# Three more weight slots from smaller rings, a gather moved behind the up product, and one branch for last passes and eviction, in a two-layer decoder trunk with a mixture of experts

## The chip, the cores and the metric

The kernel runs on one core of a Trainium2 chip. The metric is device time in microseconds: the median of the runs shown.

## The reference

Two layers; the second ends in a mixture of eight experts, of which each of 256 tokens takes two. The change touches how the expert part is run.

```python
D_MODEL, SEQ, DEPTH = 1024, 256, 2
N_EXPERTS, TOP_K, D_FF_EXPERT = 8, 2, 3584
...
def moe_swiglu(x, w_router, e_gate, e_up, e_down):
    ...
    logits = (t @ w_router).astype(jnp.float32)
    top_val, top_idx = lax.top_k(logits, TOP_K)
    top_w = jax.nn.softmax(top_val, axis=-1)
    gates = jnp.sum(jax.nn.one_hot(top_idx, N_EXPERTS, dtype=jnp.float32) * top_w[..., None], axis=1)
    out = jnp.zeros_like(t)
    for e in range(N_EXPERTS):
        out = out + gates[:, e:e + 1] * swiglu(t, e_gate[e], e_up[e], e_down[e])
    return out.reshape(B, S, D)

def reference(...):
    for layer in range(DEPTH):
        h = hybrid_mixer(x, ...)
        x = layer_norm(DEEPNORM_ALPHA * x + h, ...)
        f = swiglu(x, ...) if layer % 2 == 0 else moe_swiglu(x, ...)
        x = layer_norm(DEEPNORM_ALPHA * x + f, ...)
    return x
```

## The kernel before

All weights are float32 and come from HBM in **units** of 1 MB (128 partitions x 2048). `Stream` (name `W`) holds a plan of units in the order of use, and `NS` = 16 SBUF slots of one unit each, 18 in the expert part (`NX` = 2 more from a pool opened once the mixers' own tiles are gone). A unit is loaded into a slot (`load`, L169, on SP's queue, in order), and then `split` (L271, L272) writes it into two other slots: a rounded high part `h` by ScalarE (ACT) and the rest `l` = unit - h by VectorE (DVE). Products on TensorE (PE) use h and l in turn. `pump` decides after every step of the product loops (a `tick`; four to a unit) what is loaded and split: it splits a unit 12 ticks ahead of its use (`lead`), and it loads whenever more than 1 + max(0, freed + reserve - split) slots are idle, with reserve 5 in the expert part. So a spare slot goes to a load, not to a deeper lead of the splits. Slots come from a first-in first-out list.

An expert runs in four groups of hidden columns, 512, 1024, 1024, 1024 (the last expert the other way round). A group of 1024 has four units of gate, four of up, four of down. The first unit of each gate product is used unsplit (`whole`, L1050, against `xw`, the first half of the expert's tokens in plain float32). The order in the code is: gate product of group g, its eviction by ACT (`gated`, L1075), up product, its eviction (`finish`, L1085), and then the down product of the group *before* (`down`, L1137, L1144), so a group's hidden values have 13 ticks to be folded (L1108), activated (L1110), split (L1111 to L1113) and stored as `ch`, `cl`.

The routing is only known at run time. An expert with up to 64 tokens is narrow: its x holds high and low halves side by side in 128 columns, so that two matmuls per block do; one with more is wide and takes a third matmul (`rest`). Which one it is decides a branch (`cases`, L969) that PE, ACT and DVE all take. `last_passes` (L1032) is such a branch at the end of each pair of units; `gated` and `finish` are each another one right behind it.

Before expert e+1 starts, its tokens are picked from the residual `xf` by matmuls with a one-hot matrix: `one_hot` (L979 to L986, DVE), then `gather`: two transposes (L1012) and a copy to `pt` (L1014), then for each half of the model width a `pick` (L1000, PE), its split `exh`/`exl` (L991, L992), and the copy to `xw` (L1025). The whole is a task started after the down product inside group 2; it steps along with the ticks of the gate product of group 3. After an expert's last down product, `scatter` adds its result to `acc` (L1166 and L1167 on PE, L1169 on DVE); this falls into the first ticks of the next expert's group 1.

The numbers of tokens are such that experts 0 and 2 are wide and the other six narrow. PE starts expert 0's group 1 at 432.35 us, and the experts that follow at 536.8, 648.5, 774.5, 885.9, 995.0, 1104.5 and 1213.6 us.

Of the kernel before, what the change touches and what calls it, by code (L numbers as in the profile page):

```python
# [16 lines left out]
P = 128  # L17
# [12 lines left out]
NS = 16  # L30
NX = 2
NR = 6
# [7 lines left out]
def trunk(ctx: ExitStack, tc: tile.TileContext, x, w_in, gm_ws, gm_bs, gm_ln_g, gm_ln_b, gla_wa2, gla_ba,  # L40
# [26 lines left out]
    def tiny(name, n, dt=F32):  # L67
        return act.tile([P, n], dt, tag="tiny", name=name, bufs=10, padded_shape=[P, 32])

# [222 lines left out]
    def norm(y, st, gt, bt, nm):  # L292
# [85 lines left out]
    def transposed_parts(sg, nm, kt):  # L378

        tp = psw(f"th{nm}", (P, 4, P))  # L380
        for j in range(kt):
            nc.tensor.transpose(tp[:, j, :], sg[:, j * P:(j + 1) * P], ident)
        ch = act.tile([P, 4, P], F32R, tag="ch", name=f"ch{nm}", bufs=4)
        cl = act.tile([P, 4, P], F32R, tag="cl", name=f"cl{nm}", bufs=4)
        split(ch[:, 0:kt, :], cl[:, 0:kt, :], tp[:, 0:kt, :])
        return ch, cl
# [85 lines left out]
    def mixer(l, xT, small, ready, nxT):  # L472
# [354 lines left out]
    def moe(xT, ready, consts):  # L827
        iota, pri, ones, ecst, pair, fold, powers = consts
        lg = const.tile([P, 2, NE], F32, name="lg")
        plt = psy("plt", (P, 2, NE))  # L830
# [32 lines left out]
        small = const.tile([P, NE], F32, name="small")  # L863
        acc = [room[-1].tile([P, D], F32, name=f"acc{tb}") for tb in range(2)]

# [85 lines left out]
        class Expert:  # L951
# [22 lines left out]
            def one_hot(self):  # L974
                nm = self.nm
                self.oh = act.tile([P, 2, P], F32, tag="oh", name=f"oh{nm}", bufs=1)
                self.twice = self.oh
                for tb in range(2):
                    nc.vector.tensor_scalar(self.oh[:, tb, :], iota, self.rank(tb), None, op0=ALU.is_equal)  # L979
                if self.fewer is not None:  # L980
                    self.twice = s2(f"oh2{nm}", F32, (P, 2, P))
                    slot = s2(f"slot{nm}")[:, 0:P]
# [25 lines left out]
            def gather(self):  # L1008
# [5 lines left out]
                nc.scalar.activation(self.pt, tp, AF.Copy)  # L1014
                xh = act.tile([P, KT, P], F32R, tag="xh", name=f"exh{nm}")
                xl = act.tile([P, KT, P], F32R, tag="xl", name=f"exl{nm}")
                self.x = xh, xl
                for hf in range(2):
                    p = pst(f"gx{nm}{hf}", (P, 4, P))
                    self.pick(p, [xf[tb][:, hf * 512:hf * 512 + 512] for tb in range(2)])  # L1020
                    self.parts(xh[:, hf * 4:hf * 4 + 4, :], xl[:, hf * 4:hf * 4 + 4, :], p)
                    if hf == 0:
                        if self.wide is not None:
                            self.xw = room[-1].tile([P, 4, P], F32, tag="xw", name=f"xw{nm}", bufs=2)
                            nc.scalar.activation(self.xw, p, AF.Copy)  # L1025
                        yield 2

            def last_passes(self, rest, last):

                def run(ms):  # L1030
                    for ps, x, w, stop in ms:
                        nc.tensor.matmul(ps, x, w, start=False, stop=stop, skip_group_check=True)  # L1032
                self.cases(lambda: run(last), lambda: run([*rest, *last]))

            def product(self, units, n, nm):

# [4 lines left out]
                held, rest, last = [], [], []  # L1041
                for u, ((wh, wl), free, drop) in enumerate(units):
                    held.append(free)
                    for j in range(kk):
                        k = kk * u + j
                        for b in range(nb):
# [23 lines left out]
            def gated(self, pg, nm):  # L1070
# [8 lines left out]
            def finish(self, g, sg, pu, lag=13):  # L1079
                nm = f"e{self.nm}{g}"  # L1080
# [16 lines left out]
            def transposed(self, nm, sg, up):  # L1097

                tp = pst(f"th{nm}", (P, 4, P))
                ch = act.tile([P, 4, P], F32R, tag="ch", name=f"ch{nm}", bufs=4)  # L1100
                cl = act.tile([P, 4, P], F32R, tag="cl", name=f"cl{nm}", bufs=4)
                hid = room[-1].tile([P, 4, HALF], F32, tag="hid", name=f"hid{nm}", bufs=2)

# [91 lines left out]
        while W.hold:  # L1195
            tasks["route"].step()
        W.lead, W.reserve = LEAD_E, NC
        for i, t in enumerate((ybanks, ybanks, tbanks, tbanks)):
            t.append(psy(f"bank{i}"))

        def first_hidden():
            yield 4
            p = pst("gh", (P, 4, P))
            experts[0].pick(p, first, hidden_columns)
            ch = act.tile([P, 4, P], F32R, tag="ch", name="che0f", bufs=4)
            cl = act.tile([P, 4, P], F32R, tag="cl", name="cle0f", bufs=4)
            experts[0].parts(ch, cl, p)
# [7 lines left out]
        for e, ex in enumerate(experts):  # L1215
            for g, (c0, n) in enumerate(groups(e)):
# [4 lines left out]
                if (e, g) == (NE // 2, 1):  # L1221
                    most = nc.values_load(cnt_i[0:1, 0:1], min_val=0, max_val=2 * P)
                sg = ex.gated(ex.product(stream(gate_units(e, g)), n, f"eg{e}{g}"), f"e{e}{g}")
# [5 lines left out]
                pu = ex.product(stream(up_units(e, g)), n, f"eu{e}{g}")  # L1229
                task = Task(ex.finish(g, sg, pu, 3 if last else 13))  # L1230
                W.cap = len(W.plan) - 2 if last else len(W.plan)
# [17 lines left out]
        with tc.If(most > P):  # L1249
# [4 lines left out]
            with tc.For_i(0, NE) as ei:  # L1254
# [29 lines left out]
                for g in range(FE // 512):  # L1284
                    sg = ex.gated(ex.product(cols_of(exp_g, g), 512, f"egz{g}"), f"ez{g}")
                    pu = ex.product(cols_of(exp_u, g), 512, f"euz{g}")
                    Task(ex.finish(g, sg, pu)).finish()
                    ex.down(g, rows_of(g), g == 0, g == FE // 512 - 1)
# [112 lines left out]
```

## Time and profile before

| what | us |
|---|---|
| median of 3 runs | 1343.92 (1342.61 to 1344.07) |
| profiled execution, its own time | 1342.48 |
| its span, first to last instruction | 1340.8 |
| PE busy | 1296.5 (97%) |
| DVE busy | 1068.5 (80%) |
| ACT busy | 839.0 (63%) |
| mean HBM rate over the span | 318 GB/s |

A "PE busy" includes matmuls whose modelled ends overlap the next one's start, so PE's waits are read from the starts of its matmuls and from what the weight loads (PEld) and matmuls waited for. The mean granted TensorE clock is 0.996 of full speed. The expert part takes some 930 us of the span.

### The profile page before, as it was taken

The numbers are of one execution on the slowest core, as the hardware profiler recorded it, in microseconds if no ns is written. First come the engines' busy times: TensorE is split into PE (matmuls) and PEld (weight loads), VectorE is DVE, ScalarE is ACT, GpSimd is POOL, SyncE is SP. The second block draws the span as 40 slices with busy tenths as digits, with TensorE's granted clock in tenths as the row PEclk, the third lists the DMA queues.
The fourth block names the chain that finished last, engine by engine and source line by source line (L and its number), as shares of the span: only waits on it lengthen the run. The fifth ranks groups of instructions, "written<-read, shape, count | busy, mean of one in ns | idle before, by whom it ended". The sixth has DMA issues, their size and how long they took to land. (4 is left out here: it accounts for less than half of the span.)

```text
span 1340.8 us, 16964 instructions
## 1 busy us (share of the span) xinstructions
PE 1296.5 (97%) x6113; PEld 1024.0 (76%) x6113; DVE 1068.5 (80%) x965; ACT 839.0 (63%) x702; POOL 37.7 (3%) x79
## 2 busy tenths in 40 slices
PE   8999999999998999999999999999999999999996
PEld 7878888888887788777778877776776776777774
DVE  6687544476684887898888789899899989989997
ACT  5653444346342666687756667776777777877783
POOL 1012000000110000000000000000000000000000
PEclk9999999999999999999999999999999999999998
DMA  9636656543484598999999899999999999999993
GB/s 343 256 126 205 240 188 204 203 157 132 159 301 162 222 365 321 392 370 380 408 368 369 320 384 370 389 408 412 408 389 408 409 393 410 407 400 403 412 407 118
DMA packets 118766, 426.35 MB, mean 318 GB/s; under 512 B 8089, under 2 KB 10722, under 8 KB 104578
## 3 DMA queue, kind: packets, MB, share of 16 engines
q1 hardware_dynamic: 117218, 420.61, 81.0%
q0 software_dynamic: 1440, 4.33, 1.1%
q8 instruction: 64, 1.05, 0.3%
q14 instruction: 44, 0.36, 0.1%
HBM read 423.86 MB, written 1.05 MB: 317 GB/s over the span
## 5 line engine op out<-in xcount | busy, mean ns | idle before, releaser
L272 DVE TENSOR_TENSOR l<-r,h 128x2048 fp32r<-128x2048 f32 (+2 forms) x373 | 833.3, 2249 | 134.0 <-ACT h L271 117.6
L271 ACT ACTIVATE h<-r 128x2048 fp32r<-128x2048 f32 (+2 forms) x373 | 685.0, 1881 | 124.1 <-PE bank L1032 39.1
L1137 PE MATMUL bank<-h,che 128*128 128x512 f32 x440 | 174.4, 396 | 0.0
L1053 PE MATMUL eu<-h,exh 128*128 128x512 f32 x440 | 167.5, 389 | 0.0
L1144 PE MATMUL bank<-l,che 128*128 128x512 f32 x377 | 153.3, 407 | 7.0 <-DVEq L969 3.5
L1060 PE MATMUL eu<-l,exh 128*128 128x512 f32 x361 | 141.0, 391 | 0.3 <-DVE l L272 0.3
L1053 PE MATMUL eg<-h,exh 128*128 128x512 f32 x316 | 128.2, 418 | 0.0
L1050 PE MATMUL eg<-r,xw 128*128 128x512 f32 x248 | 114.5, 595 | 0.0
L1144 PEld LDWEIGHTS bank<-l,che 128*128 128x128 f32 x377 | 70.8, 188 | 41.9 <-DVE l L272 17.1
L1053 PEld LDWEIGHTS eu<-h,exh 128*128 128x128 f32 x440 | 82.6, 188 | 16.9
L1137 PEld LDWEIGHTS bank<-h,che 128*128 128x128 f32 x440 | 82.8, 188 | 15.2
L1060 PE MATMUL eg<-l,exh 128*128 128x512 f32 x237 | 92.7, 391 | 0.1
L1060 PEld LDWEIGHTS eu<-l,exh 128*128 128x128 f32 x361 | 67.8, 188 | 15.9 <-DVE l L272 2.1
L1050 PEld LDWEIGHTS eg<-r,xw 128*128 128x128 f32 x248 | 45.2, 190 | 39.6 <-issue 37.8
L266 PE MATMUL f<-h,xhm 128*128 128x512 f32 (+1 forms) x192 | 72.2, 376 | 0.0
L267 PE MATMUL f<-l,xhm 128*128 128x512 f32 (+1 forms) x192 | 71.4, 372 | 0.0
L268 PE MATMUL f<-h,xlm 128*128 128x512 f32 (+1 forms) x192 | 71.4, 372 | 0.0
L1053 PEld LDWEIGHTS eg<-h,exh 128*128 128x128 f32 x316 | 59.5, 188 | 15.4 <-issue 4.1
L1110 ACT ACTIVATE hide<-bank 128x256 f32<-128x256 f32 x42 | 16.1, 384 | 71.7 <-PE bank L1108 71.7
L1060 PEld LDWEIGHTS eg<-l,exh 128*128 128x128 f32 x237 | 44.6, 188 | 12.7 <-issue 3.8
L1075 ACT ACTIVATE sge<-eg 128x512 f32<-128x512 f32 x55 | 30.2, 595 | 36.4 <-PE eg L1032 36.3
L1108 PEld LDWEIGHTS bank<-fold,sge 128*128 128x128 f32 x336 | 46.0, 196 | 5.2 <-issue 2.4
(354 smaller groups left out, 1803.3 us busy)
## 6 DMA issues: line engine op xcount, KB each, us to landing
r<-in_exp_w_gate SPq DMA_DIRECT2D x112, 1024.0 KB, 11.1
r<-in_exp_w_up SPq DMA_DIRECT2D x112, 1024.0 KB, 7.5
r<-in_exp_w_down SPq DMA_DIRECT2D x110, 1024.0 KB, 11.6
r<-in_w_in SPq DMA_DIRECT2D x17, 1024.0 KB, 8.5
r<-in_ffn_w_gate SPq DMA_DIRECT2D x11, 1024.0 KB, 6.9
r<-in_ffn_w_up SPq DMA_DIRECT2D x11, 1024.0 KB, 5.3
r<-in_ffn_w_down SPq DMA_DIRECT2D x11, 1024.0 KB, 4.9
r<-in_w_out SPq DMA_DIRECT2D x8, 1024.0 KB, 9.2
```

Source lines behind the costliest of these rows:

```text
L266: nc.tensor.matmul(ps, xh, wh, start=start, stop=False)
L267: nc.tensor.matmul(ps, xh, wl, start=False, stop=False)
L268: nc.tensor.matmul(ps, xl, wh, start=False, stop=stop)
L271: nc.scalar.activation(dst_h, src, AF.Copy)
L272: nc.vector.tensor_tensor(dst_l, src, dst_h.bitcast(F32), op=ALU.subtract)
L1050: nc.tensor.matmul(p[b], self.xw[:, k, :], wh[:, j, s], start=k == 0, stop=False, skip_group_check=True)
L1053: nc.tensor.matmul(p[b], xh[:, k, :], wh[:, j, s], start=k == 0, stop=False, skip_group_check=True)
L1060: nc.tensor.matmul(*second[0:3], start=False, stop=False, skip_group_check=True)
L1075: nc.scalar.activation(o, i, f)
L1108: nc.tensor.matmul(tp[:, j, i * HALF:i * HALF + HALF], hidden_columns(t, j), fold, start=True, stop=True)
L1137: nc.tensor.matmul(y, ch[:, k, :], wh[:, j, s], start=first and u + j == 0, stop=False, skip_group_check=True)
L1144: nc.tensor.matmul(y, ch[:, k, :], wl[:, j, s], start=False, stop=False, skip_group_check=True)
```

## The change

1. **Slots.** `NX` goes from 2 to 4, so the expert part has 20 slots, and a 21st (`w20`) is lent by the slot that holds the second token block's `xh`, `xl` until the dense first products of expert 0 are done. The room comes from smaller rings: `tiny` 10 to 7; `xh`, `xl` two each to one each (`x_parts`); `xw` 2 to 1; `ch`, `cl` move to the mixers' pool before the expert part, and in it are two each, not four (`hidden_parts`); `oh` and the scatter's `yh`, `yl` come out of the shared ring `s2` of six; the fold's `hid` is written over `sg`. The pool for the extra slots is opened at the start of `moe`, no longer before the last mixer's output projection.
2. **Gather.** With one x there, the next expert's gather can't start before the last use of the present one. `one_hot` stays where it was (end of group 2's pass); `gather` is started right behind the up product of the last group and its eviction, so it steps along with the down product of group 2 instead of the gate product of group 3.
3. **Branch.** The last `last_passes` of a gate or up product and the eviction behind it become one `cases` branch (`end`).
4. **Small.** The slot of an unsplit unit is freed right after its own matmuls, not with the unit after it. The last group's fold comes 9 ticks after its up product, not 3.

```diff
-NX = 2
+NX = 4
...
-        return act.tile([P, n], dt, tag="tiny", name=name, bufs=10, padded_shape=[P, 32])
+        return act.tile([P, n], dt, tag="tiny", name=name, bufs=7, padded_shape=[P, 32])
...
+    def x_parts(nm):
+        return [act.tile([P, KT, P], F32R, tag=f"x{i}", name=f"x{i}{nm}", bufs=1) for i in "hl"]
+    def slot_parts(nm):
+        t = wt.tile([P, 2048], F32R, tag=f"w{NS + NX}", name=f"x{nm}").rearrange("p (i k n) -> p i k n", i=2, k=KT)
+        return t[:, 0], t[:, 1]
...
-        xh = act.tile([P, KT, P], F32R, tag="xh", name=f"xh{nm}{tb}")
-        xl = act.tile([P, KT, P], F32R, tag="xl", name=f"xl{nm}{tb}")
+        xh, xl = x_parts(f"{nm}{tb}") if tb == 0 else slot_parts(f"{nm}{tb}")
...
-        if l == DEPTH - 1:
-            mix_only.close()
-            more = ctx.enter_context(tc.tile_pool(name="more", bufs=1))
-            room.extend([more] * NX)
-            idle.extend(range(NS, NS + NX))
...
     def moe(xT, ready, consts):
+        mix_only.close()
+        more = ctx.enter_context(tc.tile_pool(name="more", bufs=1))
+        room.extend([more] * NX + [wt])
+        idle.extend(range(NS, NS + NX))
...
+        def hidden_parts(nm):
+            return [more.tile([P, 4, P], F32R, tag=t, name=f"{t}{nm}", bufs=2) for t in ("ch", "cl")]
...
-            def last_passes(self, rest, last):
-                def run(ms):
+            def last_passes(self, rest, last, few=None, many=None):
+                def run(ms, then):
                     for ps, x, w, stop in ms:
                         nc.tensor.matmul(ps, x, w, start=False, stop=stop, skip_group_check=True)
-                self.cases(lambda: run(last), lambda: run([*rest, *last]))
+                    if then:
+                        then()
+                self.cases(lambda: run(last, few), lambda: run([*rest, *last], many))
...
-                    if u % 2 == 0:
+                    if wl is None:
+                        free()
+                    elif u % 2 == 0:
                         drop()
-                    if u % 2 and (nb > 1 or u == 1):
-                        self.last_passes(rest, last)
-                        for free in held:
-                            free()
-                        held, rest, last = [], [], []
-                return p
+                    if u % 2 and u < KT // kk - 1:
+                        end()
+                return p, end
...
-                self.cases(lambda: all(AF.Copy), lambda: all(AF.Silu))
+                end(lambda: all(AF.Copy), lambda: all(AF.Silu))
...
-                self.cases(copies, products)
+                end(copies, products)
...
-                hid = room[-1].tile([P, 4, HALF], F32, tag="hid", name=f"hid{nm}", bufs=2)
+                ch, cl = hidden_parts(nm)
+                hid = sg[:, 0:4 * HALF].rearrange("p (a b) -> p a b", a=4)
...
-                    yh = act.tile([P, 512], F32R, tag="ch", name=f"yh{self.nm}{hf}", bufs=4)
-                    yl = act.tile([P, 512], F32R, tag="cl", name=f"yl{self.nm}{hf}", bufs=4)
+                    yh = s2(f"yh{self.nm}{hf}", F32R)
+                    yl = s2(f"yl{self.nm}{hf}", F32R)
...
         while W.hold:
             tasks["route"].step()
+        idle.append(NS + NX)
...
-                task = Task(ex.finish(g, sg, pu, 3 if last else 13))
+                pu, end = ex.product(stream(up_units(e, g)), n, f"eu{e}{g}")
+                task = Task(ex.finish(g, sg, pu, end, 9 if last else 13))
+                if g == NG - 1 and e + 1 < NE:
+                    tasks["gather", e + 1] = Task(experts[e + 1].gather())
...
                 if g == NG - 2 and e + 1 < NE:
-                    tasks["gather", e + 1] = Task(experts[e + 1].gather_from_scratch())
+                    experts[e + 1].one_hot()
```

## Rows read from the trace of the kernel before

**Rows 1.** Busy time in stretches: from the routing on, one row for each expert as PE starts it (the first is the routing with expert 0's first products). Columns: the stretch, its length, busy time of each engine with its instructions, granted clock, DMA share, GB/s.

```profile
396.00:432.35 36.35, 32.48 (x185) 27.53 (x184) 16.94 (x47) 7.74 (x12) 2.46 (x15) 0.95 0.50 183
432.35:536.80 104.45, 104.08 (x472) 82.82 (x471) 86.40 (x64) 66.88 (x48) 0.69 (x1) 1.00 0.78 302
536.80:648.50 111.70, 108.51 (x508) 83.73 (x507) 99.30 (x70) 82.44 (x65) 0.00 (x0) 1.00 0.97 383
648.50:774.50 126.00, 123.30 (x543) 97.04 (x543) 101.65 (x70) 79.86 (x58) 0.00 (x0) 1.00 0.93 364
...
885.90:995.00 109.10, 105.10 (x491) 80.61 (x491) 99.49 (x73) 81.78 (x65) 0.00 (x0) 1.00 1.01 403
```

**Rows 2.** All weight loads of the kernel (line L169): the issues of the three expert matrices (count, duration of an issue min/median/max in ns, first and last start) and who waited for a load (us, times).

```profile
L169 SPq DMA_DIRECT2D r<-in_exp_w_down x114: 327/360/882, 396.4 to 1298.3; - x114
...
who waited for it (us, times):
  ACT h L271: 11.5, 7
```

**Rows 3.** SP's queue in order of time around the start of the expert part: start, duration, what is issued, how many loads.

```profile
396.40 8.64 SPq L169 DMA_DIRECT2D r<-in_exp_w_down  x2
422.55 5.43 SPq L169 DMA_DIRECT2D r<-in_exp_w_gate  x4
449.60 6.14 SPq L169 DMA_DIRECT2D r<-in_exp_w_up  x4
```

**Rows 4.** Who waited for whom from 432 to 1335 us: engine, line, what for, us in total, times, longest.

```profile
DVE l L272 <- ACT h L271: 78.4, 66, 5.2
...
ACT h L271 <- PE bank L1032: 39.1, 24, 4.2
```

**Rows 5.** Busy time in stretches again, groups 0, 1 and 3 of expert 4 (narrow, behind a narrow one) and, last, group 1 of expert 3 (narrow, behind a wide one). Columns as in rows 1.

```profile
885.90:903.90 18.00, 18.00 (x81) 13.75 (x80) 16.19 (x12) 15.13 (x12) 0.00 (x0) 1.00 1.02 409
903.90:929.10 25.20, 22.87 (x90) 16.16 (x89) 23.70 (x18) 18.89 (x14) 0.00 (x0) 1.00 1.02 409
...
961.80:995.00 33.20, 32.15 (x164) 25.35 (x163) 29.07 (x25) 24.40 (x21) 0.00 (x0) 1.00 1.01 392
...
796.10:820.00 23.90, 22.60 (x90) 16.25 (x89) 21.22 (x14) 18.88 (x14) 0.00 (x0) 1.00 0.91 350
```

**Rows 6.** DVE in order of time through group 3 of expert 4 and into expert 5: start, duration, line, operation, how many in a row; in brackets the idle time before and what ended it.

```profile
965.05 2.28 DVE L272 TENSOR_TENSOR l<-r,h 128x2048 fp32r<-128x2048 f32 x1
967.76 0.42 DVE L992 TENSOR_TENSOR exh<-bank,exh 128x256 fp32r<-128x256 f32 x1 [0.42 <-ACT exh L991]
970.65 2.29 DVE L272 TENSOR_TENSOR l<-r,h 128x2048 fp32r<-128x2048 f32 x1 [2.46 <-ACT h L271]
...
987.78 6.88 DVE L272 TENSOR_TENSOR l<-r,h 128x2048 fp32r<-128x2048 f32 x3 [0.27 <-DVEq L969]
...
997.25 4.67 DVE L272 TENSOR_TENSOR l<-r,h 128x2048 fp32r<-128x2048 f32 x2 [0.27 <-ACT h L271]
1002.80 2.29 DVE L272 TENSOR_TENSOR l<-r,h 128x2048 fp32r<-128x2048 f32 x1 [0.87 <-ACT h L271]
```

**Rows 7.** ACT in order of time through the same group. Columns as in rows 6.

```profile
967.34 0.38 ACT L991 ACTIVATE exh<-bank 128x256 fp32r<-128x256 f32 x1 [2.27 <-DVE l L272]
968.22 0.60 ACT L1025 ACTIVATE xw<-bank 128x512 f32<-128x512 f32 x1 [0.49 <-DVE exh L992]
968.71 1.91 ACT L271 ACTIVATE h<-r 128x2048 fp32r<-128x2048 f32 x1
...
983.51 1.08 ACT L1085 ACTIVATE upe<-eu 128x512 f32<-128x512 f32 x2
```

**Rows 8.** PE in order of time in group 2 of expert 1: an unsplit unit, a fold, and the first matmul of the next unit. Columns as in rows 6.

```profile
582.29 3.60 PE L1050 MATMUL eg<-r,xw 128*128 128x512 f32 x8
585.73 1.04 PE L1108 MATMUL bank<-fold,sge 128*128 128x64 f32 x8
...
587.52 0.47 PE L1053 MATMUL eg<-h,exh 128*128 128x512 f32 x1
```

**Rows 9.** PE in order of time in group 3 of expert 4: the unsplit unit with the gather in it, two matmuls of one run (14 starts apart), the last passes of the up product, and the first matmuls of expert 5. Columns as in rows 6.

```profile
961.64 2.79 PE L1050 MATMUL eg<-r,xw 128*128 128x512 f32 x6
964.27 0.38 PE L1012 MATMUL bank<-ident,oh 128*128 128x128 f32 x2
965.28 2.02 PE L1000 MATMUL bank<-oh,xin 128*128 128x128 f32 x16 [0.63 <-DVE che L1113]
967.14 1.02 PE L1050 MATMUL eg<-r,xw 128*128 128x512 f32 x2
...
971.18 0.39 PE L1053 MATMUL eg<-h,exh 128*128 128x512 f32 x1
...
974.38 0.61 PE L1053 MATMUL eg<-h,exh 128*128 128x512 f32 x2
...
982.08 0.62 PE L1032 MATMUL eu<-l,exh 128*128 128x512 f32 x2
...
994.83 1.51 PE L1050 MATMUL eg<-r,xw 128*128 128x512 f32 x3
```

**Rows 10.** The branches of `cases` (line L969): records on each engine's queue, duration min/median/max in ns.

```profile
L969 DVEq COMPARE_BRANCH  x382: 43/56/69, 417.5 to 1320.7; - x191
L969 PEldq COMPARE_BRANCH  x382: 65/202/350, 418.0 to 1324.6; - x191
```

More of the change, by code (lines that the diff above doesn't have):

```diff
@@ L382, in transposed_parts @@
             nc.tensor.transpose(tp[:, j, :], sg[:, j * P:(j + 1) * P], ident)
-        ch = act.tile([P, 4, P], F32R, tag="ch", name=f"ch{nm}", bufs=4)
-        cl = act.tile([P, 4, P], F32R, tag="cl", name=f"cl{nm}", bufs=4)
+        ch = mix.tile([P, 4, P], F32R, tag="ch", name=f"ch{nm}", bufs=4)
+        cl = mix.tile([P, 4, P], F32R, tag="cl", name=f"cl{nm}", bufs=4)
         split(ch[:, 0:kt, :], cl[:, 0:kt, :], tp[:, 0:kt, :])
@@ L863, in moe @@
         small = const.tile([P, NE], F32, name="small")
-        acc = [room[-1].tile([P, D], F32, name=f"acc{tb}") for tb in range(2)]
+        acc = [more.tile([P, D], F32, name=f"acc{tb}") for tb in range(2)]
+        def hidden_parts(nm):
+            return [more.tile([P, 4, P], F32R, tag=t, name=f"{t}{nm}", bufs=2) for t in ("ch", "cl")]
         def routing():
@@ L975, in one_hot @@
                 nm = self.nm
-                self.oh = act.tile([P, 2, P], F32, tag="oh", name=f"oh{nm}", bufs=1)
+                if self.fewer is not None:
+                    slot = s2(f"slot{nm}")[:, 0:P]
+                self.oh = s2(f"oh{nm}", F32, (P, 2, P))
                 self.twice = self.oh
@@ L981, in one_hot @@
                     self.twice = s2(f"oh2{nm}", F32, (P, 2, P))
-                    slot = s2(f"slot{nm}")[:, 0:P]
                     nc.vector.tensor_scalar(slot, iota, HALF - 0.5, self.fewer, op0=ALU.is_ge, op1=ALU.mult)
@@ L1014, in gather @@
                 nc.scalar.activation(self.pt, tp, AF.Copy)
-                xh = act.tile([P, KT, P], F32R, tag="xh", name=f"exh{nm}")
-                xl = act.tile([P, KT, P], F32R, tag="xl", name=f"exl{nm}")
-                self.x = xh, xl
+                self.x = xh, xl = x_parts(f"e{nm}")
                 for hf in range(2):
@@ L1023, in gather @@
                         if self.wide is not None:
-                            self.xw = room[-1].tile([P, 4, P], F32, tag="xw", name=f"xw{nm}", bufs=2)
+                            self.xw = more.tile([P, 4, P], F32, tag="xw", name=f"xw{nm}", bufs=1)
                             nc.scalar.activation(self.xw, p, AF.Copy)
                         yield 2
-            def last_passes(self, rest, last):
-                def run(ms):
+            def last_passes(self, rest, last, few=None, many=None):
+                def run(ms, then):
                     for ps, x, w, stop in ms:
                         nc.tensor.matmul(ps, x, w, start=False, stop=stop, skip_group_check=True)
-                self.cases(lambda: run(last), lambda: run([*rest, *last]))
+                    if then:
+                        then()
+                self.cases(lambda: run(last, few), lambda: run([*rest, *last], many))
             def product(self, units, n, nm):
@@ L1041, in product, with end @@
                 held, rest, last = [], [], []
+                def end(few=None, many=None):
+                    self.last_passes(rest, last, few, many)
+                    for free in held:
+                        free()
+                    for t in (held, rest, last):
+                        t.clear()
                 for u, ((wh, wl), free, drop) in enumerate(units):
-                    held.append(free)
+                    if wl is not None:
+                        held.append(free)
                     for j in range(kk):
@@ L1060, in product, with gated @@
                                 nc.tensor.matmul(*second[0:3], start=False, stop=False, skip_group_check=True)
-                    if u % 2 == 0:
+                    if wl is None:
+                        free()
+                    elif u % 2 == 0:
                         drop()
-                    if u % 2 and (nb > 1 or u == 1):
-                        self.last_passes(rest, last)
-                        for free in held:
-                            free()
-                        held, rest, last = [], [], []
-                return p
-            def gated(self, pg, nm):
+                    if u % 2 and u < KT // kk - 1:
+                        end()
+                return p, end
+            def gated(self, pg, end, nm):
                 t = [s2(f"sg{nm}{b}") for b in range(len(pg))]
@@ L1075, in all, with finish @@
                         nc.scalar.activation(o, i, f)
-                self.cases(lambda: all(AF.Copy), lambda: all(AF.Silu))
+                end(lambda: all(AF.Copy), lambda: all(AF.Silu))
                 return t
-            def finish(self, g, sg, pu, lag=13):
+            def finish(self, g, sg, pu, end, lag=13):
                 nm = f"e{self.nm}{g}"
@@ L1099, in transposed @@
                 tp = pst(f"th{nm}", (P, 4, P))
-                ch = act.tile([P, 4, P], F32R, tag="ch", name=f"ch{nm}", bufs=4)
-                cl = act.tile([P, 4, P], F32R, tag="cl", name=f"cl{nm}", bufs=4)
-                hid = room[-1].tile([P, 4, HALF], F32, tag="hid", name=f"hid{nm}", bufs=2)
+                ch, cl = hidden_parts(nm)
+                hid = sg[:, 0:4 * HALF].rearrange("p (a b) -> p a b", a=4)
                 def few():
@@ L1204, in first_hidden @@
             experts[0].pick(p, first, hidden_columns)
-            ch = act.tile([P, 4, P], F32R, tag="ch", name="che0f", bufs=4)
-            cl = act.tile([P, 4, P], F32R, tag="cl", name="cle0f", bufs=4)
+            ch, cl = hidden_parts("e0f")
             experts[0].parts(ch, cl, p)
@@ L1222, in moe @@
                     most = nc.values_load(cnt_i[0:1, 0:1], min_val=0, max_val=2 * P)
-                sg = ex.gated(ex.product(stream(gate_units(e, g)), n, f"eg{e}{g}"), f"e{e}{g}")
+                sg = ex.gated(*ex.product(stream(gate_units(e, g)), n, f"eg{e}{g}"), f"e{e}{g}")
                 if (e, g) == (0, 1):
@@ L1284, in moe @@
                 for g in range(FE // 512):
-                    sg = ex.gated(ex.product(cols_of(exp_g, g), 512, f"egz{g}"), f"ez{g}")
-                    pu = ex.product(cols_of(exp_u, g), 512, f"euz{g}")
-                    Task(ex.finish(g, sg, pu)).finish()
+                    sg = ex.gated(*ex.product(cols_of(exp_g, g), 512, f"egz{g}"), f"ez{g}")
+                    pu, end = ex.product(cols_of(exp_u, g), 512, f"euz{g}")
+                    Task(ex.finish(g, sg, pu, end)).finish()
                     ex.down(g, rows_of(g), g == 0, g == FE // 512 - 1)
```

1 line of the change is left out of this document (removed).

## The prediction

> **What bounds the kernel now.** I read the stretches by expert first. In the wide experts 0 and 2 PE is busy nearly throughout (104.08 of 104.45, 123.30 of 126.00 us) while DMA is not full (302 and 364 GB/s): PE sets the pace. A narrow expert such as 4 takes 109.10 us with PE busy 105.10, DVE 99.49 and DMA at 403 GB/s: three resources lie within some per cent [rows 1]. So I asked next who waits. For weights nobody does in the expert part: all waits for a load come to 11.5 us, as often as 7 times [rows 2], and the waits from 432 us on name no DMA at all; what they name is DVE waiting for ACT's high part (78.4 us) and ACT waiting for PE to be done with a slot that it writes (39.1 us) [rows 4]. Idle DMA is there too: after a load at about 405 us the next issue is at 422.55, and after four more at 449.60 [rows 3]. That is prefetch standing with all slots full; nothing later waits for it.
>
> Then the order of time in one narrow group. DVE splits back to back, a unit in 2.29 us (6.88 for three), and its gaps all stand where ACT had waited for PE: at the gather (0.42 and 2.46 us) and behind evictions (0.27, 0.87) [rows 6]. PE starts a matmul every 0.2286 us (3.20 us for 14) [rows 9], eight to a unit, 1.83 us; an unsplit unit takes 3.44 and a fold 1.79 us [rows 8]. A unit costs PE less than DVE; folds, unsplit units and the gather let DVE catch up. Neither is alone the bound: PE and DVE hand the end back and forth. Wide experts hide DVE entirely.
>
> **The slots.** They add three loads of lookahead. The code gives spare slots to loads, and no split waits for a load, so their direct worth is nothing; the lead of the splits (12 ticks, reserve 5) is untouched. While the last output projection runs, two slots fewer are there than before; I take it that the loads put off go out with the new slots near 397 us, where the first load of a down unit is issued now (396.40, [rows 3]). They are for expert 0's group 1, which PE doesn't start before 432.35 [rows 1]; seven loads of 1.05 MB at 409 GB/s [rows 5] are through by 397 + 7 x 2.56 = 415. Hidden, with 17 us to spare; without that cover each late load would cost up to 2.56. The indirect worth: an expert moves 42 units, 44.04 MB, which at 409 GB/s takes 107.7 us. If a narrow expert falls below that, loads begin to bind, and three more units (7.7 us) carry it over.
>
> The Trainium skill, page "Perfetto Trace Analysis", section "Optimization Strategy", says that one gap repeating on a busy engine can mean that there is too little SBUF for the next tile. By it the 39.1 us of ACT waiting for slots would go, and the time would be near 1305. That is the third rival.
>
> **The gather.** Per expert it costs PE two transposes (0.25 us) and two picks (1.86 each, from 965.28 to 967.14), 4.0 us, plus 0.63 waiting for a bank that a fold still holds [rows 9]; that work stays, and only its place changes. I follow group 3 of expert 4 with these durations. PE starts at 961.64. Without the gather: 3.44 + 7 x 1.83 gives 977.9 for the end of the up product. DVE starts its first split at 965.05 [rows 6]; eight in a row, now without the gaps, end at 983.4. The fifth ends at 976.5, where PE wants it at 976.3, so PE is done at 978.1 (now 982.5, [rows 9]). Now comes the gather: first pick done 980.2, one tick, second pick done 982.5, eleven ticks (5.0), fold, last down unit, fold: 993.0. Before, the next expert starts at 994.83 [rows 9]: **1.8 us saved**, since PE does the gather while DVE is catching up.
>
> DVE's side must allow it. Before, it comes to the point behind the up product 5.0 us after PE (987.5 against 982.5) [rows 6, 9]. After: at 983.7, with the 0.27 for the branch. There it finds the pick done, writes exh, and the next split starts 2.89 us later, as from 967.76 to 970.65 now [rows 6]: ACT's xw, then its h, come between. That split, for the last down unit, ends at 988.9; PE wants it at 989.5. The gap of some 2.5 us on DVE thus stays, at another place. What goes are the gaps behind: PE comes 1.8 us earlier to the evictions that held ACT (0.27 and 0.87), so that DVE also is some 1.9 us ahead when expert 5 begins its group 1.
>
> The xw copy now waits 0.49 us for DVE's exh, which reads the same bank [rows 7]. In the new place DVE is late, so ACT is held longer, from about 981 to 984; the 2.89 us have that hold in them.
>
> Seven gathers move. Those inside wide experts 0 and 2 lie where PE is full already: 0. Five are inside narrow ones (1, 3, 4, 5, 6): 5 x 1.8 = **9.0 us**. Bounds per gather: at best 3.1, if group 1 also takes 23.90 instead of 25.20 us, as it does behind a wide expert, where DVE had time to catch up [rows 5]; at worst a loss of 0.7 (last rival).
>
> **The branch.** Thirty-one groups with two products each: 62 branches fewer. A record takes 0.056 us on DVE and 0.202 on PE's queue [rows 10]. They run ahead under a split of 2.29 us, or while ACT waits; PE's last passes, two in 0.62 us, show no gap [rows 9]. Value 0; exposed on DVE it is 62 x 0.056 = 3.5 us gain. Against it, up to 0.23 us (one matmul) if the first eviction now waits for the second last pass: 62 of these are 14 us, nearly all under the 2.29 us splits; I take 0, and 3 us as the outer end, five narrow experts by eight evictions at a third exposed.
>
> The Trainium skill, "Advanced Engine Details and Errata", section "Control Flow Timing", gives a compare-and-branch about 108 ns; by it 62 would be worth 6.7 us if bare, for a time near 1337 alone. The records here differ (0.056, 0.202).
>
> **The small edits.** An unsplit slot freed four ticks earlier, hid written over sg (ACT waited for that fold anyway), oh, yh and yl from `s2` (four of its six are long done when the scatter comes; if a late one is taken, yh waits for DVE's hidden part), two `ch`, `cl` (their readers end five ticks before): 0, and up to 0.5 a scatter, 3.5 in all, the wrong way. The last fold at tick 9: between -0.7 and +0.7; 0.
>
> **Sum.** On the profiled execution's own time, 1342.48 (span 1340.8): 1342.48 - 9.0 = 1333.5. The median lies 1.44 above that execution: 1343.92 - 9.0 = **1334.9**.
>
> **Rivals.** (1) Forecast, about 1335. For it: DVE's lag of 5 us. Chance 0.47.
> (2) More: the scatter wait goes as well, 4 x 1.3 for experts 4 to 7. 1343.92 - 9.0 - 5.2 = 1329.7. Against it: DVE is ahead by no more than PE is. 0.11.
> (3) Slots free ACT: all 39.1 us of waits for slots [rows 4] go and lie on the path, 1304.8. Against it: spare slots go to loads in the code, and DVE's gaps in rows 6 stand at the gather and behind evictions. 0.02.
> (4) The branches were bare: gain of 3.5 alone, 1340.4. 0.07.
> (5) Nothing: the gap on DVE is only carried from the gate product to the down product, and as DVE is the tighter one no time is won; slots unread. 1343.9. For it: DVE's 2.5 us gap remains. 0.20.
> (6) Slower: the gather sits behind an eviction, and ACT can do no split until pick, exh and xw are through. It decides by DVE's lag at the end of the up product: exh can't come before 2.5 us after it (0.25, 1.86 and exh's 0.38), so each us that the lag falls short of 2.5 is lost; under 0.7 us the gain of 1.8 is gone. With no lag each of the five loses 0.7: 1343.92 + 3.5 = 1347.4. Against it: the lag of 5.0. 0.13.
>
> **How the numbers follow.** About 0.2%, 2.7 us, is what a measurement here can tell. Faster: 0.44 of case 1, cases 2, 3 and 4, 0.02 of case 5, together 0.66; slower: case 6 and 0.02 of case 5, 0.15; the rest, 0.19, the same. The range leaves out case 3, most of case 6 and the far ends: below, case 2 less 2.7 us; above, case 5 plus 1: 1327 to 1345. The forecast's own range is 1330 to 1341.
>
> **What would show it.** Right: group 3 of experts 3 to 6 near 31.4 us instead of 33.20, groups 1 and 2 unchanged; transposes and picks behind the up product's last passes; DVE idle some 2.5 us before the first split there; PE without a wait in that down product; loads issued between 405 and 422 us; HBM near 410 GB/s in narrow experts; experts 0 and 2 as long as before. Wrong: a wait of PE for the last down unit's l, a group 0 that gives the gain back, yh waiting for the hidden part on DVE, or a wait for a weight DMA.

## The result and the profile after

The changed kernel takes 1357.25 us (median of 4 runs, 1355.97 to 1357.89) against 1343.26 of the kernel before on the same chip: 1.0103 times as long, 95% interval 1.0085 to 1.012. Forecast were 1334.9 and a gain; it is a loss of 14 us. The profiled execution has a span of 1355.7 us.

The stretches of the changed kernel by PE's starts, as in [rows 1] and [rows 5]: routing, experts 0, 1, 2 and 4, then groups 0 to 3 of expert 4. Columns as there.

```profile
396.00:434.89 38.89, 34.98 (x200) 29.60 (x198) 18.14 (x48) 9.56 (x14) 2.45 (x15) 0.96 0.79 305
434.89:539.16 104.27, 104.27 (x471) 82.85 (x470) 86.30 (x64) 66.75 (x48) 0.70 (x1) 1.00 0.84 325
539.16:651.74 112.58, 109.01 (x508) 83.65 (x507) 98.11 (x69) 81.98 (x65) 0.00 (x0) 1.00 0.94 372
651.74:778.63 126.89, 124.24 (x544) 97.17 (x544) 102.70 (x72) 79.63 (x58) 0.00 (x0) 1.00 0.94 366
891.60:1002.32 110.72, 105.91 (x492) 80.50 (x492) 99.35 (x74) 81.24 (x65) 0.00 (x0) 1.00 1.00 398
891.60:911.10 19.50, 18.85 (x83) 13.83 (x82) 16.94 (x14) 15.06 (x12) 0.00 (x0) 1.00 0.97 380
911.10:936.30 25.20, 22.91 (x90) 16.14 (x89) 23.66 (x18) 18.75 (x14) 0.00 (x0) 1.00 0.98 385
936.30:968.50 32.20, 31.86 (x162) 25.29 (x160) 30.37 (x20) 23.50 (x19) 0.00 (x0) 1.00 1.02 411
968.50:1002.32 33.82, 32.28 (x164) 25.24 (x164) 28.38 (x25) 23.93 (x21) 0.00 (x0) 1.00 1.02 405
```

The wide experts are as long as before (0) or some 0.8 us longer (2). The narrow ones lose more, 1.6 us in expert 4 (110.72 against 109.10), and DMA is less full there (398 GB/s against 403). The last expert, which has its groups the other way round, loses most: from PE's first matmul in it to the end of the span are 131.4 us, before 127.4. DVE does the same work (99.35 against 99.49 us busy), so it idles longer. Group 3, which was to fall to 31.4 us, takes 33.82; group 0 has grown from 18.00 (18.16 by PE's first matmuls, as in the table further down) to 19.50.

The expert part starts 2.5 us later. Of that, 1.7 us are there by 45 us of the span, and they belong to this execution: PE had waited 0.93 us for the input until 10.50 us, and was then granted a clock of 0.55 (most of the stretch at its lower level, 1.2 GHz) where the kernel before had 1.00:

```profile
11.00:14.50 3.50, 3.50 (x13) 2.97 (x13) 2.01 (x3) 2.79 (x4) 0.00 (x0) 0.55 1.08 323
```

No other profile of a kernel made from this one has that dip. It doesn't explain the loss: the four runs lie within 2 us, and from the start of the expert part on the changed kernel takes 920.8 us against 908.4.

Who waited for whom from 432 to 1335 us in the changed kernel, as in [rows 4]:

```profile
ACT h L271 <- DVE l L272: 106.1, 33, 5.4
DVE l L272 <- ACT h L271: 92.1, 68, 5.1
...
ACT h L271 <- PE bank L1043: 22.2, 14, 4.3
PEld eu L1082 <- DVE l L272: 18.2, 21, 1.7
```

The first row is new at this size: before, that wait came to 6.0 us in 4 times. ACT's high part waits for DVE's low part, which is the wrong way round: within a unit DVE waits for ACT. It can only be the low part of another unit. ACT's wait for slots that PE still reads has shrunk (39.1 to 22.2), and PE now waits for DVE's low part in the up products (18.2 us, before 2.1).

DVE, ACT and PE in order of time in group 3 of expert 4, as in [rows 6], [rows 7] and [rows 9]:

```profile
971.87 4.67 DVE L272 TENSOR_TENSOR l<-r,h 128x2048 fp32r<-128x2048 f32 x2
978.52 13.84 DVE L272 TENSOR_TENSOR l<-r,h 128x2048 fp32r<-128x2048 f32 x6 [1.98 <-ACT h L271]
992.70 0.42 DVE L1004 TENSOR_TENSOR xhe<-bank,xhe 128x256 fp32r<-128x256 f32 x1 [0.34 <-DVEq L980]
995.59 2.29 DVE L272 TENSOR_TENSOR l<-r,h 128x2048 fp32r<-128x2048 f32 x1 [2.46 <-ACT h L271]
...
1011.69 2.29 DVE L272 TENSOR_TENSOR l<-r,h 128x2048 fp32r<-128x2048 f32 x1 [1.99 <-ACT h L271]
```

```profile
968.98 3.71 ACT L271 ACTIVATE h<-r 128x2048 fp32r<-128x2048 f32 x2
976.57 3.72 ACT L271 ACTIVATE h<-r 128x2048 fp32r<-128x2048 f32 x2 [3.88 <-DVE l L272]
...
993.15 0.60 ACT L1035 ACTIVATE xw<-bank 128x512 f32<-128x512 f32 x1 [3.18 <-DVE xhe L1004]
```

```profile
980.86 0.50 PE L1082 MATMUL eu<-l,xhe 128*128 128x512 f32 x1 [1.18 <-DVE l L272]
...
985.44 0.50 PE L1082 MATMUL eu<-l,xhe 128*128 128x512 f32 x1 [0.26 <-DVE l L272]
...
986.69 0.63 PE L1043 MATMUL eu<-l,xhe 128*128 128x512 f32 x2
987.15 0.38 PE L1024 MATMUL bank<-ident,oh 128*128 128x128 f32 x2
987.37 1.95 PE L1012 MATMUL bank<-oh,xin 128*128 128x128 f32 x16
```

ACT has done two high parts by 972.69 and then stands still for 3.88 us, until DVE ends its second low part (971.87 + 4.67 = 976.54). Only then does it make the third, in 1.9 us, and DVE waits 1.98 us for that. The two engines, which otherwise work on different units, take turns once. It comes again at 1011.69, in the next expert's group 0. The gather is where it was to be, behind the up product's last passes, with the gap of 2.46 us on DVE.

In the code, a split hands its raw slot back to the list of idle slots when it is emitted, and the next slot asked for is the first of that list. If the next h gets it, ACT must wait for the low part that still reads it. The order in which the program hands out slots while it is built shows where that happens. Before, the slot of an unsplit unit (213, say) is freed with its neighbour's after the last passes: four slots are idle, a load takes the one that split 217 has just read, and h of 218 gets that of 213. With the early free the slot of 213 comes alone, one tick earlier; two idle slots are enough for a split and too few for a load, and the first of the two is the one that split 217 is reading. Followed through the whole code, the list does this in 30 of the 31 groups of the experts. The trace agrees: 33 waits of the kind, against 4 before. The expectations below count only 22; that number is too small. That was the theory for the runs.

### The profile page after: what moved, and what is told of

It is laid out like the page before. It is cut to its first block, busy times and chain, and to the rows that moved or that the text cites. A ratio compares the mean times of both kernels' runs of the same rounds, so it can differ in the third digit from the quotient of the medians.

```text
span 1355.7 us, 16718 instructions
## 1 busy us (share of the span) xinstructions
PE 1306.5 (96%) x6113; PEld 1025.4 (76%) x6113; DVE 1068.3 (79%) x965; ACT 836.2 (62%) x702; POOL 37.5 (3%) x79
## 5 line engine op out<-in xcount | busy, mean ns | idle before, releaser
L1075 PE MATMUL eu<-h,xhe 128*128 128x512 f32 x440 | 167.8, 390 | 0.0
L1082 PE MATMUL eu<-l,xhe 128*128 128x512 f32 x361 | 143.3, 397 | 9.2 <-DVE l L272 8.7
L1075 PE MATMUL eg<-h,xhe 128*128 128x512 f32 x316 | 127.7, 416 | 0.0
L1075 PEld LDWEIGHTS eu<-h,xhe 128*128 128x128 f32 x440 | 82.6, 188 | 16.8
L1082 PE MATMUL eg<-l,xhe 128*128 128x512 f32 x237 | 92.8, 392 | 0.0
L1082 PEld LDWEIGHTS eu<-l,xhe 128*128 128x128 f32 x361 | 67.7, 188 | 32.1 <-DVE l L272 18.2
L1075 PEld LDWEIGHTS eg<-h,xhe 128*128 128x128 f32 x316 | 59.4, 188 | 15.8 <-issue 4.1
L1082 PEld LDWEIGHTS eg<-l,xhe 128*128 128x128 f32 x237 | 44.6, 188 | 12.9 <-issue 2.6
L1128 PE MATMUL bank<-fold,upe 128*128 128x64 f32 x336 | 46.4, 281 | 0.0
L1128 PE MATMUL bank<-fold,sge 128*128 128x64 f32 x336 | 43.8, 273 | 0.0
```

Source lines behind the costliest of these rows:

```text
L1075: nc.tensor.matmul(p[b], xh[:, k, :], wh[:, j, s], start=k == 0, stop=False, skip_group_check=True)
L1128: nc.tensor.matmul(tp[:, j, i * HALF:i * HALF + HALF], hidden_columns(t, j), fold, start=True, stop=True)
```

## The experiments

**The unsplit slot freed with its pair again**, all else as in the changed kernel:

```
-                    if wl is not None:
-                        held.append(free)
+                    held.append(free)
...
-                    if wl is None:
-                        free()
-                    elif u % 2 == 0:
+                    if u % 2 == 0:
                         drop()
```

> The changed kernel, in which only the unsplit slot of a gate product is freed with its pair again, as before. Theory (slot order): with the slot freed four ticks earlier, a split can start one tick earlier, when the head of the list of idle slots is the slot that DVE's l of the unit just before still reads; ACT's h waits for that l, then DVE waits some 1.9 us for h, once a group (22 times by the order in which slots are handed out). Without it ACT h <- DVE l falls from 127.9 us to near 28, and the time from 1357 to 1334 to 1341 (all of the forecast's gain, or all but the 2.5 us lost ahead of 434 us and a gather that gains less). Rival A (the gather in its new place is what costs): 1352 to 1357, and ACT h <- DVE l stays. Rival B (more slots, or the pool opened later): 1354 to 1357.

Measured 1338.58 us (ratio to the kernel before 0.997, 0.9958 to 0.9983), 18.7 less than the changed kernel. From 432 us on:

```profile
DVE l L272 <- ACT h L271: 71.8, 54, 5.2
...
ACT h L271 <- DVE l L272: 5.8, 4, 1.9
```

The wait is back to its size before (6.0 us, 4 times) with one edit; gather, rings, slots and branches, still in it, are not what costs.

**The early free alone**, on the kernel before:

```
-                    held.append(free)
+                    if wl is not None:
+                        held.append(free)
...
-                    if u % 2 == 0:
+                    if wl is None:
+                        free()
+                    elif u % 2 == 0:
                         drop()
```

> The kernel before, in which only the unsplit slot of a gate product is freed as soon as its passes are issued; 18 slots, gather and branches as before. Theory (slot order): 22 splits again write h into the slot that l of the unit before reads; DVE loses up to 1.9 us in each, of which some 15 lie in narrow experts: 1350 to 1364. Rivals A and B: 1342 to 1345, since nothing that they blame is in it.

Measured 1355.53 us against 1343.16 (1.0097, 1.0082 to 1.0113): 12.4 us slower, from an edit costed at nothing.

```profile
DVE l L272 <- ACT h L271: 97.4, 78, 5.1
ACT h L271 <- DVE l L272: 93.5, 33, 5.4
```

**The early free kept, h and l changing slots.** This leaves every tick, load and split of the changed kernel where it is; only where the first idle slot is the one just read, l takes it (DVE writes there what it has itself read) and h takes the other:

```
+            if idle[0] == self.read:
+                idle.insert(1, idle.pop(0))
             h, sh = self.slot(f"h{i}", F32R, a, b)
             l, sl = self.slot(f"l{i}", F32R, a, b)
...
             idle.append(slot)
+            self.read = slot
```

> The changed kernel with its early free, ticks and loads, where only this is added: if the first idle slot is the one that the split just before has read, h and l of the next unit change slots (l, which DVE writes itself, takes the slot just read). Theory (slot order): 1332 to 1341, as with the slot freed with its pair or a little better, since splits keep their earlier tick; ACT h <- DVE l near 28 us. Rivals A and B: 1352 to 1357. If it is the earlier tick itself and not the slot that costs: 1350 to 1357 as well, while the run with the slot freed with its pair is fast.

Measured 1335.85 us (0.9948, 0.9934 to 0.9962): 21.4 us less than the changed kernel.

```profile
DVE l L276 <- ACT h L275: 72.2, 47, 5.2
...
ACT h L275 <- DVE l L276: 7.3, 4, 3.3
```

So it is the slot and not the tick. The earlier tick is even worth something: 2.7 us against the first run, though the two intervals overlap a little.

**The price by its number.** The kernel before, made to give h the slot just read also where it is second in the list:

```
+            if len(idle) > 1 and idle[1] == self.read:
+                idle.insert(0, idle.pop(1))
```

> The kernel before, with nothing else changed than that h takes the slot just read by the split before it wherever it is second in the list (l takes the other): 99 splits by the order in which slots are handed out, against 22 with the early free. Theory (a price per such split): 22 cost 12.4 us, so 99 cost 56 us at least, and up to 1.9 us for each of some 75 in narrow experts, 140: 1399 to 1485. If the price is not that of the slot but of the tick: 1341 to 1346.

Measured 1541.78 us (1.1476), 199 more than before, well over the upper end.

This run ends at 1541 us. Who waited for whom from 432 us to there:

```profile
ACT h L275 <- DVE l L276: 374.5, 127, 6.4
DVE l L276 <- ACT h L275: 268.3, 165, 5.1
```

```profile
619.33 4.49 DVE L276 TENSOR_TENSOR l<-r,h 128x2048 fp32r<-128x2048 f32 x2 [1.98 <-ACT h L275]
625.80 2.29 DVE L276 TENSOR_TENSOR l<-r,h 128x2048 fp32r<-128x2048 f32 x1 [1.98 <-ACT h L275]
```

It is the same gap of 1.98 us on DVE. Some 11 of the 199 us lie ahead of the expert part, since the edit acts there too; the other 188 over 123 more waits than before are 1.5 us each. With the early free it is 12.4 us over 29 more waits, 0.4 each: one in a group seems to be made good in part by the slack of the group, four are not. Not all of the 1.5 us need be the wait itself. PE, which waits for DVE's low part here, is granted a mean clock of 0.94 over this expert part (2.4 GHz with stretches at 1.2), where it had 1.00 in the experts before; the run doesn't separate the two. The 99 splits of the expectation were too few, which is one reason that it came out too low.

```profile
443.50:1541.40 1097.90, 953.10 (x3991) 709.76 (x3989) 796.98 (x589) 646.61 (x507) 2.67 (x3) 0.94 0.80 307
```

**The gather alone**, on the kernel before:

```
+                if g == NG - 1 and e + 1 < NE:
+                    tasks["gather", e + 1] = Task(experts[e + 1].gather())
                 W.cap = len(W.plan) - 2 if last else len(W.plan)
...
-                    tasks["gather", e + 1] = Task(experts[e + 1].gather_from_scratch())
+                    experts[e + 1].one_hot()
```

> The kernel before, in which only the gather is moved: one hot matrices behind group 2, gather behind the eviction of group 3's up product; 18 slots, rings, frees and branches as before. The forecast's step: 9.0 us less, 1335 (1333 to 1338), group 3 of narrow experts near 31.4 us. Rival A (gather in its new place holds ACT and DVE at a worse point): 1345 to 1352.

Measured 1334.81 us against 1343.16 (0.9937, 0.9923 to 0.995): 8.35 us less, where 9.0 were forecast. Group 3 of expert 4 in it, and DVE there:

```profile
958.70:990.16 31.46, 31.38 (x164) 25.41 (x164) 27.99 (x25) 24.07 (x21) 0.00 (x0) 1.00 1.03 408
882.74:900.89 18.15, 18.15 (x83) 13.91 (x82) 17.24 (x14) 15.13 (x12) 0.00 (x0) 1.00 1.02 408
```

```profile
962.12 18.43 DVE L272 TENSOR_TENSOR l<-r,h 128x2048 fp32r<-128x2048 f32 x8
980.89 0.42 DVE L992 TENSOR_TENSOR exh<-bank,exh 128x256 fp32r<-128x256 f32 x1 [0.34 <-DVEq L969]
983.78 2.29 DVE L272 TENSOR_TENSOR l<-r,h 128x2048 fp32r<-128x2048 f32 x1 [2.47 <-ACT h L271]
```

Eight splits in a row, where the changed kernel has two, a gap and six. PE is busy 31.38 of 31.46 us.

**The shared branch alone**, on the kernel before (the last passes of a product and the eviction in one `cases`, for the gate product likewise):

```
-                self.cases(copies, products)
+                end(copies, products)
```

> The kernel before, in which only the last passes of a gate or up product share the branch of the eviction behind them. Stretches of the runs so far, with this edit against without it, are 0.25 to 0.35 us longer in each group of the wide experts 0 and 2 and up to 0.2 in groups 0 and 1 of narrow ones. If that is the shared branch (PE's last pass or the eviction held): 1345 to 1347. The forecast's value, nothing: 1342.5 to 1344. If the branches were bare and their saving lies on the path: 1340.4.

Measured 1344.48 us against 1342.88 (1.0007, 0.9998 to 1.0016). That lies between the ranges for a cost and for nothing: no gain, and a loss of 2 us at most, none certain. The longer groups of the wide experts are not in this run (group 2 of expert 0: 35.36 us, as before), so they are not the branch's.

**Gather, early free and exchanged slots**, on the kernel before, with 18 slots and the old rings (the three diffs above together):

> The kernel before with the moved gather, the early free, and h and l changing slots where the first idle slot is the one just read; 18 slots, rings and branches as before. Theory: the early free is worth something once h no longer takes the slot that l is reading (2.7 us between the two repaired forms of the changed kernel): 1334.8 - 2.5 = 1332 (1330.5 to 1333.5). If the early tick is worth nothing in itself: 1334 to 1336.

Measured 1333.35 us (0.9921, 0.9908 to 0.9935), at the upper end of the theory's range: the earlier tick may be worth 1.5 us here, which the intervals don't separate from nothing. By expert it brings more and loses some of it again: against the gather alone the first seven experts take 4.5 us less together, and the last one 2.2 us more (130.05 against 127.81), where ACT now waits 7.4 us for weight loads. With 18 slots the loads have begun to bind there.

**The changed kernel with exchanged slots, branches apart again**:

```
-                end(copies, products)
+                end()
+                self.cases(copies, products)
```

> The changed kernel with h and l changing slots (1335.85 measured), in which the last passes and the evictions have their own branches again, as before; 21 slots and smaller rings stay. If the shared branch costs 2 to 3 us: 1333 to 1334. If what is left against the kernel before with three edits alone lies in the slots, rings or the pool opened later: 1335 to 1336.5. With 21 slots worth nothing either way it should come out level with that kernel.

Measured 1334.82 us (0.9939, 0.9925 to 0.9952). It lies between the two cases, 1.0 below the run with shared branches and 1.5 above the one with 18 slots, and the intervals separate it from neither. In sum, three more slots used for loads alone are worth nothing. That sum hides two parts: the last expert takes 127.81 us again, without a wait of ACT for loads, 2.2 less than with 18 slots; the other seven take 3.2 us more together, with the wider matmul spacing told at the end.

**The same with the slots given to splits**:

```
-NC = 5
+NC = 6
...
-LEAD_E = 12
+LEAD_E = 16
```

> The same kernel (changed, slots exchanged, branches separate), in which the three more slots are given to splits instead of loads: lead of the splits 16 ticks for 12, reserve 6 units for 5. If DVE's and ACT's distance to PE is what the narrow experts lack: 2 to 6 us under the run without it, ACT h <- PE bank under 15 us. If DVE's own work is the bound there, or PE's: within 1.5 us of the run without it.

Measured 1329.95 us (0.9897, 0.9882 to 0.9912), 4.9 under the run without it and the fastest of all. Expert 4 takes

```profile
882.19:988.59 106.40, 104.24 (x493) 82.14 (x492) 98.98 (x74) 81.52 (x65) 0.00 (x0) 0.98 1.02 410
```

which is less than the 107.7 us that its loads were estimated to take at 409 GB/s: the lookahead carries the rest over from the wide experts. ACT's wait for slots that PE reads stays at 28.1 us, against the expectation's 15; the gain comes with the splits a unit ahead, not with that wait. What goes is PE's own wait for the low part: the PEld rows name 12.5 us of it in the run without the longer lead, and 0.5 us here.

**The same lead on 18 slots** (the same two constants in the kernel with three edits), and **a lead of 20 ticks and 7 units on 21** (`LEAD_E = 20`, `NC = 7` in the run just told):

> The kernel before with moved gather, early free and slots exchanged (1333.35 measured with a lead of 12 ticks and 5 units), with a lead of 16 ticks and 6 units on its 18 slots. If the gain of the same step on 21 slots (4.9 us) comes from the splits running a unit further ahead and needs no more room: 1327 to 1330. If three loads fewer ahead let transfers come late: 1333 or above, with waits for weight DMAs.

> The changed kernel with slots exchanged and separate branches, lead 20 ticks and 7 units on 21 slots. If the distance of the splits still binds: 1326 to 1329. If PE or DVE is now the bound: within 1.5 us of 1329.95; if loads come late: above 1332.

Measured 1347.8 us (1.0043, 1.0029 to 1.0057; runs from 1343.9 to 1352.8) and 1334.42 us (0.9943, 0.993 to 0.9956). In the first, ACT waits for transfers:

```profile
ACT h L275 <- DMA r<-in_exp_w_gate: 24.6, 24, 2.5
ACT h L275 <- DMA r<-in_exp_w_up: 15.4, 25, 1.1
ACT h L275 <- DMA r<-in_exp_w_down: 10.6, 22, 0.7
```

With 21 slots and a lead of 16 these rows come to 8 us, with a lead of 20 to 18. So the three slots are what the longer lead needs, and a lead of 20 eats them up. (The run on 18 slots also has the rings of before, whose matmul spacing, told at the end, is the narrower one.)

**Memory between slots and rings**, in the kernel with three edits:

```
-NX = 2
+NX = 1
...
+    space = wt.tile([P, 1024], F32, tag="space", name="space")
+    nc.gpsimd.memset(space[:, 0:1], 0.0)
```

> In every run with the changed rings and 21 slots a matmul follows the one before it in 0.2297 us on average in group 2 of expert 0, against 0.2276 in every run with the rings of before. Here three edits on the kernel before (1333.35), 17 slots, and an unused 4 KB of each partition between the weight slots and the rings, which moves all rings. If the place of the rings in memory makes the difference: a spacing near 0.229 in that stretch. If it is which tiles lie beside which, or the loads running: 0.2276.

Measured 1336.79 us (2 runs; 0.9955, 0.9938 to 0.9972), and a spacing of 0.2276 us: moving the rings by 4 KB does not bring the wider spacing. With one slot fewer than 18 it is 3.4 us slower than the kernel it was made from.

## Why the prediction was wrong

**The step that failed** stands among the small edits: "An unsplit slot freed four ticks earlier ... : 0, and up to 0.5 a scatter, 3.5 in all, the wrong way". Alone that edit costs 12.4 us, and in the changed kernel 18.7 to 21.4, because it also takes the gather's gain. I costed the free as an event that nobody waits for. I did not ask who gets the slot, and at which place in the list it comes. The code for that was in front of me: the list is served from its head, and a raw slot is put back when the split is issued, while ACT and DVE still have to read it.

By group of expert 4, from PE's first matmul of one group to that of the next, in us:

| group | before | changed | early free alone | gather alone | changed, freed in pair |
|---|---|---|---|---|---|
| 0 | 18.16 | 19.50 | 19.18 | 18.14 | 18.31 |
| 1 | 25.18 | 25.20 | 25.17 | 25.25 | 25.38 |
| 2 | 32.56 | 32.20 | 32.18 | 32.57 | 32.60 |
| 3 | 33.19 | 33.83 | 34.45 | 31.46 | 31.51 |
| sum | 109.09 | 110.73 | 110.98 | 107.42 | 107.80 |

Read the early free alone against before: it gives 0.4 in group 2 and costs 1.0 in group 0 and 1.3 in group 3. With it, the gather's 1.7 us in group 3 shrink to 0.6 (34.45 to 33.83). PE's new waits for the low part suggest that DVE, not PE, then sets the end of the group.

**The gather** was right, in mechanism and size. It was to bring 1.8 us in each of five narrow experts. By the group 3 of experts 1, 3, 4, 5 and 6 it is 2.0, 1.8, 1.7, 1.7 and 1.7, together 8.8, and the median says 8.35. DVE's first exh was put at 983.7 with PE starting at 961.64, 22.1 us into the group; it came at 980.89 - 958.70 = 22.2. The split behind it was to start 2.89 us later, and did (983.78). Group 0 does not give the gain back when the gather stands alone.

**The slots.** Nothing for loads alone, as forecast (1334.82 with 21, 1333.35 with 18). The hedge on them was right too: loads begin to bind once a narrow expert falls below 107.7 us. In the kernel with three edits expert 4 takes 106.70, and the 18 slots then cost 2.2 us in the last expert. With the longer lead, the time is 1347.8 us on 18 slots and 1329.95 on 21. That the code gives spare slots to loads was only half of it: which slot is left for the next split was the other half. The loads put off were early enough. They go out like this (SP's queue, as in [rows 3]), the first nine up to 426 us and so later than the forecast's 415, but no wait for a load is on record near PE's start at 434.89:

```profile
398.49 9.08 SPq L169 DMA_DIRECT2D r<-in_exp_w_up  x3
407.88 0.81 SPq L169 DMA_DIRECT2D r<-in_exp_w_down  x2
408.75 17.25 SPq L169 DMA_DIRECT2D r<-in_exp_w_gate  x4
429.63 22.70 SPq L169 DMA_DIRECT2D r<-in_exp_w_up  x4
```

**The branch.** Nothing, as forecast, to within 2 us. The records on each engine's queue fall from 382 in [rows 10] to 306. These 76 fit the 62 branches of the forecast if a branch leaves two records in a wide expert (14 of the 62) and one in a narrow one:

```profile
L980 DVEq COMPARE_BRANCH  x306: 43/56/63, 420.1 to 1336.8; - x153
```

By the Trainium skill's 108 ns ("Advanced Engine Details and Errata", "Control Flow Timing") 62 branches bare would have been worth 6.7 us, as an estimate; the run with that edit alone shows none of it.

**The rivals.** The rivals that gave the gather more (a scatter's wait goes as well) or nothing are answered by the run with the gather alone, 8.35 us. The slower one, ACT held by the gather, had the direction and the wrong mechanism: ACT is held 3.18 us for the xw copy (993.15), as long as the forecast had it, and in the run with the gather alone 3.40 us, with the gain in place. The third, that slots free ACT of its 39.1 us, doesn't hold: 28 to 31 us stay in the repaired kernels. The Trainium skill's rule that a repeating gap may mean too little SBUF ("Perfetto Trace Analysis", "Optimization Strategy") agrees in one point, the 4.9 us of the longer lead. It gives no hint at the gap found here, which comes with the early free on 18 slots as on 21.

**What stays open.** The sum of the parts is not closed to a microsecond: the repaired kernel (1335.85) is 2.5 us above the one with three edits alone, of which slower matmuls (below) and the shared branch may each be a part. The last group's later fold and the other small edits were not run alone.

## What to carry to other kernels

A slot handed back at issue is free for the program and not yet for the engines: when a ring or a free list changes by one entry, follow who takes the next entry and who reads it last. Where two engines work on neighbouring units, let the engine that has read a slot last be the first to write it. More buffers bring time when the work that is on the path is allowed to run further ahead with them; count the loads' lookahead that this takes away.

## What the runs showed of the hardware

PE's matmuls came at a slightly wider spacing in every kernel with the changed rings. Group 2 of expert 0, where PE is busy throughout at a granted clock of 1.00, took 35.36 us in all seven such kernels with the rings of before (the one with 127 waits left out), and 35.62 to 35.71 in all six with the changed ones; the mean of some 129 spacings between neighbouring matmuls in it is 0.2276 us against 0.2296 to 0.2303. The instructions are the same. From the first matmul of the dense feed-forward's down projection to the first of the routing it is 0.65 us in 243 (242.42 against 243.08). An unused 4 KB ahead of the rings (35.36) doesn't bring it about, nor does a longer lead of the splits with the rings of before (35.36); what does is open.
